# Six direct pairs instead of four in three feed-forwards of a decoder trunk, with slots handed on by age, two low parts moved to VectorE, and a norm's last squares added later

## The chip, the cores and the metric

The kernel runs on one core of one Trainium2 chip. The metric is the device time of one execution in microseconds (us); lower is better. The kernel before takes 1963.95 us, the median of 3 runs (1963.61 to 1965.31).

## What is computed

A two-layer decoder trunk on one sequence of 512 tokens with 1024 channels, in float32. Each layer is feed-forward, token mixer, feed-forward, each added to x behind a norm:

```python
def rms_norm(x, g):
    y = x * lax.rsqrt(jnp.mean(x * x, axis=-1, keepdims=True) + NORM_EPS)
    return y * g

def swiglu_ffn(x, g, w_in, w_out):          # w_in 1024 x 5632, w_out 2816 x 1024
    h = rms_norm(x, g)
    gate, up = jnp.split(h @ w_in, 2, axis=-1)
    return (jax.nn.silu(gate) * up) @ w_out

for layer in range(2):
    x = x + 0.5 * swiglu_ffn(x, ffn1_norm[layer], ffn1_w_in[layer], ffn1_w_out[layer])
    x = x + mixer(x)     # layer 0: retention beside dilated attention ("hybrid"); layer 1: stick-breaking ("stick")
    x = x + 0.5 * swiglu_ffn(x, ffn2_norm[layer], ffn2_w_in[layer], ffn2_w_out[layer])
return rms_norm(x, final_norm)
```

## The kernel before

**Layout and precision.** x is kept transposed in eight tiles `x[c]` of 128 channels x 512 tokens. Every operand of a matmul is cut in two parts, hi (a cast) and lo (what the cast left over), and a product is three matmuls: hi x hi, hi x lo, lo x hi (`mm3`). `split` makes hi on ScalarE (line 206) and lo on VectorE (line 207). Weights come by a DMA from SP's queue into a slot of the role `wraw`, and their two parts stand in two slots of the role `whl` (`weight`).

**Slots and roles.** The on-chip memory has 43 slots m0 to m42, of which `WSLOTS` (0 to 9) belong to the weights: four for `wraw`, six for `whl`. `give(role=[...])` hands a role a list of slots and starts its turn at 0; `B(shape, dtype, role)` takes the next slot in turn, and what is written there waits until the slot's last reader is done. Six `whl` slots hold three cut weights.

**Order.** Instructions are put in order ahead of time by a scheduler that goes by program order as priority; `tc.high_priority(offset=n)` moves a block ahead. Between `order["on"] = True` and `False` TensorE's instructions keep the order of the code. Each engine and each DMA queue then runs its list in that order.

**The stages.** A first feed-forward (`ffn`), `hybrid`, then three times `ffn_seven` and its output projection, with `stick` ahead of the third. "First, second and third stage" below are the three calls of `ffn_seven`, which begin near 625, 977 and 1594 us and end where the output projection begins, near 854, 1218 and 1831 us.

- `ffn_seven` computes the 22 gate tiles and 22 up tiles (128 channels each) and gate x up. The first `DIRECT` = 4 pairs are direct: for each f a gate tile into a bank of the kind `acc` (`pg`, three banks) and an up tile into one of the kind `att` (`pu`, four banks), each 24 matmuls of 512 columns on h. Their eight weights are the input `wd`. Those with an index in `BYDMA` (5, 6, 7: the up weights of f = 1, 2, 3) get lo from `weight_dma`: ScalarE casts hi and then writes -hi into lo, and an accumulating DMA from POOL's queue adds the source to it. h is x times a gain, not yet normalized; the norm's factor r (`rr`) is applied to the products. It needs the sum of squares `ss` and one matmul with `ones_ms` (`norm_r`), which stands behind the first gate tile.
- `normed_forms` makes on VectorE and ScalarE the seven sums of quarters of the normalized x (T3, T1, T4, B11, T2, B22, B21) that the quads multiply.
- The other 18 pairs run as 9 quads (`quad`): two pairs at a time, with their weights in four blocks a11, a12, a21, a22 (input `wq`), by seven products instead of eight. A product is 24 matmuls of 256 columns. The order is p3 x T3, p1 x T1, a22 x T4, a11 x B11, p2 x T2, p4 x B22, a12 x B21, where p1 to p4 are sums of blocks on VectorE. p1 to p4 are cut by `cut_form` (ScalarE and VectorE); a22, a11 and a12 by `cut_raw`, which like `weight_dma` gets lo from an accumulating DMA of POOL's queue (lines 459 to 461). For the quads `wraw` has `WSLOTS[:4]` and three more slots, and `whl` has `WSLOTS[4:]` and four slots of h.
- `out_ffn` multiplies by `w_out` in eight tiles d, each in three pieces of weights (p = 0, 8, 15). Between the pieces `cut_ahead` loads a later mixer's weight, cuts it and stores both parts to DRAM ("a cut ahead"). n cuts are spread over the eight tiles, 12 in the first projection and 16 in the second and the third (that of the layer-0 `ffn2` is the second). After each tile x[d] is updated and `norm_chunk` makes h[d] (hi on ScalarE, lo on VectorE) and adds its square to `ss`.
- `out_second` is the last part of a mixer's output projection: four tiles at a time, in two passes over its three input chunks. It too ends in `norm_chunk`.

Of the kernel before, what the change touches and what calls it, by code (L numbers as in the profile page):

```python
# [30 lines left out]
GN_EPS = 1e-5  # L31


@with_exitstack
def trunk(ctx: ExitStack, tc: tile.TileContext, a: dict, out: bass.AP):
# [18 lines left out]
    home = {"h": list(range(10, 18))}  # L54

# [191 lines left out]

    def norm_chunk(c, gcol, ss):
        norm_h(c, gcol)
        norm_sum(c, ss)  # L250
# [11 lines left out]
    def norm_r(ss, epsr=None):  # L262
        ps = PS("po")
        mm(ps, ones_ms, ss, start=True, stop=True)
        r = rstd(ps, NORM_EPS, eps_n, "r")
        if epsr is not None:
            nc.vector.tensor_scalar(out=epsr, in0=ps, scalar1=NORM_EPS, scalar2=GN_EPS, op0=ALU.add, op1=ALU.mult)
        return r
# [31 lines left out]
    def out_ffn(w_out, us, gcol, ahead, n):  # L300

        ss = norm_start()
        act_set(LNEXP)
        for d in range(KC):
            ps = ACC()
            m = n * (d + 1) // KC - n * d // KC
            out_tile(w_out[d], ps, us, then=lambda p: cut_ahead(*ahead.pop(0)) if p in (8, 15)[2 - m:] else None)
            add_half(d, ps)
            norm_chunk(d, gcol, ss)
        return ss  # L310
# [61 lines left out]
    def out_second(wb, chunks, gcol):  # L372

        ss = norm_start()
        for d0 in range(0, KC, 4):
            ws = [unit((wb, d0 // 2 + i), 768) for i in range(2)]
            ps = [ATT() for _ in range(4)]
            for f in ((0, 1), (2,)):
                for i in range(4):
                    for g in f:  # L380
                        mm3(ps[i], ws[i // 2], (i % 2) * 384 + g * P, chunks[5 + g][:, 0, :], chunks[5 + g][:, 1, :],
                            g == 0, g == 2)
            for i in range(4):
                nc.vector.tensor_add(out=x[d0 + i], in0=ps[i], in1=x[d0 + i])
                norm_chunk(d0 + i, gcol, ss)
        return ss
# [39 lines left out]
    DIRECT, FORMS_AT = 4, 3  # L426
    FIRST, BYDMA = 40, (5, 6, 7)
# [53 lines left out]
    def weight_dma(src, cols):  # L481
        raw = B((P, 1024), F32, "wraw")
        hi, lo = (B((P, 1024), F32R, "whl")[:, :cols] for _ in range(2))
        nc.sync.dma_start(raw[:, :cols], src)
        nc.scalar.copy(out=hi, in_=raw[:, :cols])
        nc.scalar.mul(out=lo, in_=f32(hi), mul=-1.0)
        nc.gpsimd.dma_start(lo, src, accum_op=ALU.add)
        return hi, lo

    def quad(wq, fm, uq):  # L490

# [14 lines left out]
        w = cut_raw(a22, wq[3])  # L506
# [3 lines left out]
        w = cut_raw(a11, wq[0])  # L510
# [27 lines left out]
    def ffn_seven(ss, wd, wq, gcol, ahead=[]):  # L538
# [8 lines left out]
        for f in range(DIRECT):  # L547
# [3 lines left out]
            else:  # L551
                w2 = [weight_dma(wd[i], D) if i in BYDMA else weight(wd[i], D) for i in (f, DIRECT + f)]
            pg = ACC()
            proj_tile(None, pg, w2[0])
            if f == 0:
                rr = norm_r(ss)
                act_set(SILU)
# [4 lines left out]
            pu = ATT()  # L562
            proj_tile(None, pu, w2[1])
# [5 lines left out]
            if f == FORMS_AT:  # L569
                fm = normed_forms(rr, gcol, ext + late[3:])  # L570
        give(wraw=WSLOTS[:4] + ext[:3], p3=ext[3:], whl=WSLOTS[4:] + old[4:])
        for q in range((FC - DIRECT) // 2):
            uqs.append(B((P, 2, SEQ), F32, "uq"))
            quad(wq[q], fm, uqs[-1])
        order["on"] = False
        give(u=forms + ext + old[4:])
# [5 lines left out]
        give(wraw=WSLOTS[:4], whl=WSLOTS[4:])  # L582
# [574 lines left out]
def _layout(i):  # L1157
# [21 lines left out]
    for n, w in enumerate((g("ffn2_w_in")[0], g("ffn1_w_in")[1], g("ffn2_w_in")[1])):  # L1179
        c = cols(w)  # L1180
        o[f"wd{n}"] = np.concatenate([c[:4], c[FC:FC + 4]])

        c = c.reshape(2, FC, P, 2, 512)[:, 4:].reshape(2, FC // 2 - 2, 2, P, 2, 512)
        o[f"wq{n}"] = np.ascontiguousarray(c.transpose(1, 0, 4, 3, 2, 5).reshape(FC // 2 - 2, 4, P, 2, 512))
# [52 lines left out]
```

## Time and profile before

| | |
|---|---|
| median of 3 runs | 1963.95 us (1963.61 to 1965.31) |
| the profiled execution | 1965.91 us, of which the span is 1964.2 us |
| instructions | 29107 |
| HBM | 296.58 MB read, 67.11 MB written, 185 GB/s over the span |
| accumulating DMAs of `wq`, POOL's queue | 81, of 512 KB |
| `wraw<-wq` / `wraw<-wd` / `wraw<-f_out`, SP's queue | 108 / 24 / 102 |

All rows shown here come from that one profiled execution. Times are in microseconds from the start of the span. A row of an engine's timeline reads: start, duration, engine, line, operation, output<-inputs, shape, how many of them in a row, and in brackets how long the engine stood idle before it and what ended that. A row of the chain that ended last reads: start, duration, what it spent the time on. A row of a table by windows reads: the window, its length, busy time of TensorE (PE), its weight load (PEld), VectorE (DVE), ScalarE (ACT) and GpSimd (POOL) with the number of instructions, then the granted clock of TensorE, the share of the DMA engines and GB/s. Ends of matmuls are modelled: the last of a row of them has a tail of some 0.16 us.

### The profile page before, as it was taken

Reading aid. Unit: us, or ns where it says so; the run is one execution under the profiler, and the core shown is the slowest. Engines: PE = TensorE matmul, PEld = TensorE weight load, DVE = VectorE, ACT = ScalarE, POOL = GpSimd, SP = SyncE. Lnnn points to the kernel's source line nnn. Section 1 sums busy time; section 2 is a strip of 40 time slices with the busy share of each in tenths; the row PEclk is TensorE's granted clock in tenths of the full one; section 3 lists DMA queues with packets and bytes.
Section 4 is the critical chain, followed back from the end, with each engine's and each line's share of the span. In section 5 each row is a group of like instructions: output and inputs, shape, how many; then the busy total and the mean of one; then the engine's idle time right before and its main releaser. Section 6 shows DMA issues by size and latency. Waiting matters only on the chain.

```text
span 1964.2 us, 29107 instructions
## 1 busy us (share of the span) xinstructions
PE 1927.4 (98%) x11288; PEld 1708.9 (87%) x11288; DVE 1270.2 (65%) x1809; ACT 1002.3 (51%) x1442; POOL 145.0 (7%) x260
## 2 busy tenths in 40 slices
PE   9999999999999999999998999999999998999998
PEld 7878888888887899988778999888889878999887
DVE  7565544347767976765476677443888877677534
ACT  5344333223566566663355667343666655666523
POOL 0000000001000011100001110000222200111000
PEclk9999999999999999999999999999999999999999
DMA  7787767877533777668757766878555455777433
GB/s 245 268 290 241 257 228 251 296 254 240 177 108 104 180 172 199 161 203 295 267 173 172 199 164 151 277 245 271 162 171 159 142 146 144 199 172 170 110 91 119
DMA packets 120362, 386.57 MB, mean 197 GB/s; under 512 B 14624, under 2 KB 16288, under 8 KB 120224
## 3 DMA queue, kind: packets, MB, share of 16 engines
q1 hardware_dynamic: 107120, 337.27, 51.8%
q0 software_dynamic: 12960, 47.19, 14.0%
q8 instruction: 88, 1.44, 0.3%
q14 instruction: 50, 0.41, 0.1%
q10 hardware_dynamic: 144, 0.26, 0.0%
HBM read 296.58 MB, written 67.11 MB: 185 GB/s over the span
## 4 chain that ended last, share of the span: by engine, by line
PE 82%; DMA 7%; DVE 5%; issue 3%; ACT 2%; POOL 0%; SPq 0%; DVEq 0%; ACTq 0%; POOLq 0%
PE acc L120 42%; PE att L120 38%; PE po L120 2%; DVE whl L207 2%; DMA wraw<-f_out 1%; DMA cut_sb_k<-whl 1%; DMA whl<-wq 1%; ACT whl L206 1%; DMA wraw<-hyb_g 1%; DMA wraw<-hyb_rq 1%; DMA cut_sb_q<-whl 1%; DMA wraw<-wd 1%; DMA centred<-wraw 1%; DMA cut_sb_v<-whl 0%; PE att L123 0%
## 5 line engine op out<-in xcount | busy, mean ns | idle before, releaser
L206 ACT CAST whl<-wraw 128x1024 fp32r<-128x1024 f32 (+4 forms) x323 | 316.6, 991 | 492.3 <-PE acc L120 198.4
L207 DVE TENSOR_TENSOR whl<-wraw,whl 128x1024 fp32r<-128x1024 f32 (+4 forms) x323 | 369.7, 1151 | 303.1 <-ACT whl L206 247.4
L120 PE MATMUL acc<-u,whl 128*128 128x512 f32 (+1 forms) x2244 | 483.5, 377 | 2.0 <-DVE whl L207 2.0
L120 PEld LDWEIGHTS acc<-u,whl 128*128 128x128 f32 x2244 | 403.2, 188 | 81.0 <-DVE whl L207 3.7
L120 PE MATMUL att<-fT,whl 128*128 128x256 f32 x2592 | 324.0, 285 | 12.1 <-DMA whl<-wq 11.4
L120 PEld LDWEIGHTS att<-fT,whl 128*128 128x128 f32 x2592 | 318.6, 194 | 13.0 <-DMA whl<-wq 11.8
L120 PE MATMUL acc<-h,whl 128*128 128x512 f32 x1248 | 303.2, 393 | 6.2 <-DVE whl L207 2.9
L120 PEld LDWEIGHTS acc<-h,whl 128*128 128x128 f32 x1248 | 232.6, 188 | 60.9 <-DVE h L238 5.3
L120 PE MATMUL att<-fB,whl 128*128 128x256 f32 x1944 | 242.4, 283 | 0.0
L120 PEld LDWEIGHTS att<-fB,whl 128*128 128x128 f32 x1944 | 237.6, 192 | 0.0
L120 PE MATMUL att<-h,whl 128*128 128x512 f32 x816 | 197.7, 395 | 3.6 <-DMA whl<-wd 3.6
L120 PEld LDWEIGHTS att<-h,whl 128*128 128x128 f32 x816 | 155.1, 190 | 38.7 <-DMA whl<-wd 4.0
L459 ACT CAST whl<-wraw 128x1024 fp32r<-128x1024 f32 x81 | 84.9, 1049 | 86.3 <-PE att L120 86.3
L461 POOL DMA_DIRECT2D whl<-wq x81 | 70.1, 866 | 498.6 <-ACT whl L460 263.4
L120 PE MATMUL acc<-h,wraw 128*128 128x512 f32 x432 | 104.8, 391 | 0.0
L120 PEld LDWEIGHTS acc<-h,wraw 128*128 128x128 f32 x432 | 80.0, 188 | 16.1
L207 DVE TENSOR_TENSOR whl<-p,whl 128x1024 fp32r<-128x1024 f32 x27 | 33.1, 1225 | 88.1 <-ACT whl L206 88.1
L460 ACT ACTIVATE whl<-whl 128x1024 fp32r<-128x1024 f32 x81 | 85.9, 1060 | 2.4
L936 POOL TENSOR_SCALAR_AFFINE_SELECT t<-t 128x128 f32<-128x128 f32 x128 | 46.3, 384 | 191.3 <-DVE t L953 125.1
L102 ACT ACTIVATE t<-t 128x512 f32<-128x512 f32 (+1 forms) x91 | 51.6, 587 | 6.7 <-DVE t L789 4.2
L297 DVE SCALAR_TENSOR_TENSOR x<-acc,x 128x512 f32<-128x512 f32 (+1 forms) x34 | 22.4, 659 | 48.8 <-PE acc L120 48.7
L206 ACT CAST whl<-p 128x1024 fp32r<-128x1024 f32 x27 | 28.3, 1048 | 48.4 <-PE att L120 33.0
(183 smaller groups left out, 2146.8 us busy)
## 6 DMA issues: line engine op xcount, KB each, us to landing
wraw<-wq SPq DMA_DIRECT2D x108, 512.0 KB, 5.5
whl<-wq POOLq DMA_DIRECT2D x81, 512.0 KB, 6.6
wraw<-f_out SPq DMA_DIRECT2D x68, 448.0 KB, 4.3
wraw<-f_in SPq DMA_DIRECT2D x42, 512.0 KB, 4.7
wraw<-f_out SPq DMA_DIRECT2D x34, 512.0 KB, 4.5
wraw<-wd SPq DMA_DIRECT2D x24, 512.0 KB, 4.3
cut_sb_q<-whl SPq DMA_DIRECT2D x16, 512.0 KB, 4.4
cut_sb_k<-whl SPq DMA_DIRECT2D x16, 512.0 KB, 4.8
```

Of the source, the lines that this page charges most:

```text
L102: r = nc.scalar.activation(out=o, in_=i, func=f, **kw)
L120: return ordered(nc.tensor.matmul(*args, **kw))
L206: nc.scalar.copy(out=hi, in_=src)
L207: nc.vector.tensor_tensor(out=lo, in0=src, in1=f32(hi), op=ALU.subtract)
L297: nc.vector.scalar_tensor_tensor(out=x[d][:, sl], in0=ps[:, sl], scalar=0.5, in1=x[d][:, sl], op0=ALU.mult, op1=ALU.add)
L459: nc.scalar.copy(out=hi, in_=raw)
L460: nc.scalar.mul(out=lo, in_=f32(hi), mul=-1.0)
L461: nc.gpsimd.dma_start(lo, src, accum_op=ALU.add)
L936: nc.gpsimd.affine_select(out=t[:, at:at + P], in_=t[:, at:at + P], pattern=[[1, P]], compare_op=ALU.is_gt, fill=0.0, base=0, channel_mult ...
```

## The change

- `DIRECT` goes from 4 to 6: six pairs are direct, and eight quads are left. The weights are laid out to match (`_layout`).
- `BYDMA` is empty and `weight_dma` is gone: every direct weight is cut by `weight`.
- In quad 0 of each call (`early`) a22 and a11 are cut by `cut_form` instead of `cut_raw`. a12 keeps `cut_raw`.
- Before the quads, and for `u` and the weights behind them, a role's slots are handed on in the order in which they come free (`oldest`) instead of from the first on.
- In `norm_chunk` the squares of the last four tiles are not added there but put on a list (`pending`), which `norm_r` works off.
- In `ffn_seven` the first up tile comes before `norm_r`.
- In `out_ffn` the n cuts ahead are spread over the first seven tiles, up to three in one; the last has none.
- In `out_second` the second four tiles go through all three chunks one after the other, and their update and h come with high priority.

```diff
+DIRECT = 6
...
+    def oldest(role):
+        n = turn_of[role] % len(roles[role])
+        return roles[role][n:] + roles[role][:n]
...
+    pending = []
+
     def norm_chunk(c, gcol, ss):
         norm_h(c, gcol)
-        norm_sum(c, ss)
+        if c < KC - 4:
+            norm_sum(c, ss)
+        else:
+            pending.append((c, ss))
...
     def norm_r(ss, epsr=None):
+        while pending:
+            norm_sum(*pending.pop(0))
         ps = PS("po")
...
         for d in range(KC):
             ps = ACC()
-            m = n * (d + 1) // KC - n * d // KC
-            out_tile(w_out[d], ps, us, then=lambda p: cut_ahead(*ahead.pop(0)) if p in (8, 15)[2 - m:] else None)
+            m = n * (d + 1) // (KC - 1) - n * d // (KC - 1) if d < KC - 1 else 0
+            out_tile(w_out[d], ps, us, then=lambda p: cut_ahead(*ahead.pop(0)) if p in (0, 8, 15)[3 - m:] else None)
...
-            for f in ((0, 1), (2,)):
+            for f in ((0, 1), (2,)) if d0 == 0 else ((0, 1, 2),):
...
             for i in range(4):
-                nc.vector.tensor_add(out=x[d0 + i], in0=ps[i], in1=x[d0 + i])
-                norm_chunk(d0 + i, gcol, ss)
+                with tc.high_priority(offset=2 * FIRST if d0 else 0):
+                    nc.vector.tensor_add(out=x[d0 + i], in0=ps[i], in1=x[d0 + i])
+                    norm_chunk(d0 + i, gcol, ss)
...
-    DIRECT, FORMS_AT = 4, 3
-    FIRST, BYDMA = 40, (5, 6, 7)
+    FIRST, BYDMA = 40, ()
...
-    def quad(wq, fm, uq):
+    def quad(wq, fm, uq, early):
+        raw = (lambda t, src: cut_form(t)) if early else cut_raw
...
-        w = cut_raw(a22, wq[3])
+        w = raw(a22, wq[3])
...
-        w = cut_raw(a11, wq[0])
+        w = raw(a11, wq[0])
...
             pg = ACC()
             proj_tile(None, pg, w2[0])
             if f == 0:
+                pu = ATT()
+                proj_tile(None, pu, w2[1])
                 rr = norm_r(ss)
                 act_set(SILU)
...
-            if f == FORMS_AT:
-                fm = normed_forms(rr, gcol, ext + late[3:])
-        give(wraw=WSLOTS[:4] + ext[:3], p3=ext[3:], whl=WSLOTS[4:] + old[4:])
+            if f == DIRECT - 1:
+                fm = normed_forms(rr, gcol, ext + late[DIRECT // 2:])
+        give(wraw=oldest("wraw") + ext[:3], p3=ext[3:], whl=oldest("whl") + old[4:])
         for q in range((FC - DIRECT) // 2):
             uqs.append(B((P, 2, SEQ), F32, "uq"))
-            quad(wq[q], fm, uqs[-1])
+            quad(wq[q], fm, uqs[-1], q == 0)
         order["on"] = False
-        give(u=forms + ext + old[4:])
+        ring, raws = oldest("whl"), oldest("wraw")
+        give(u=forms + [i for i in raws + ring if i not in WSLOTS] + ext[3:])
...
-        give(wraw=WSLOTS[:4], whl=WSLOTS[4:])
+        give(wraw=[i for i in raws if i in WSLOTS], whl=[i for i in ring if i in WSLOTS])
```

How the order of instructions moves, at three places. Numbers behind a name tell one tile from another and differ between the kernels.

TensorE at the start of the third stage, around the norm's matmul `po<-ss,ones_ms`; `acc` is the first gate tile (`pg`), `att` the first up tile (`pu`). Before:

```order
L120 MATMUL acc_15163<-h_15138,whl_15153 128x512
L120 MATMUL acc_15163<-h_15145,whl_15152 128x512 x2
L120 MATMUL acc_15163<-h_15145,whl_15153 128x512
L120 MATMUL po_15188<-ss_15000,ones_ms 128x512
L120 MATMUL att_15204<-h_15050,whl_15158 128x512 x2
```

Now:

```order
L126 MATMUL att_14978<-h_14934,whl_14949 128x512
L126 MATMUL att_14978<-h_14938,whl_14948 128x512 x2
L126 MATMUL att_14978<-h_14938,whl_14949 128x512
L126 MATMUL po_15015<-ss_14802,ones_ms 128x512
L126 MATMUL acc_15047<-h_14852,whl_15036 128x512 x2
```

The norm's matmul moved from behind the first gate tile to behind the first up tile.

ScalarE where the third stage goes from the direct tiles to quad 0. The casts of p3 and p1 come first, then the silu of the last direct pair (`t<-tp`), then the blocks: before, `wraw_15512` is a11 and `wraw_15513` is a22; now `wraw_15450` is a11 and `wraw_15451` is a22. Before:

```order
L206 CAST whl_15525<-p_2548_15519 128x1024
L206 CAST whl_15556<-wraw_15511 128x1024
L102 ACTIVATE t_15414<-tp_15412 128x512
L459 CAST whl_15616<-wraw_15512 128x1024
L460 ACTIVATE whl_15617<-whl_15616 128x1024
L459 CAST whl_15586<-wraw_15513 128x1024
L460 ACTIVATE whl_15587<-whl_15586 128x1024
```

Now, and with it VectorE's list at the same place (second fence), in which `p_2588` and `wraw_15680` are the sums p3 and p1 of quad 1:

```order
L212 CAST whl_15463<-p_2559_15457 128x1024
L212 CAST whl_15494<-wraw_15449 128x1024
L108 ACTIVATE t_15352<-tp_15350 128x512
L212 CAST whl_15553<-wraw_15450 128x1024
L212 CAST whl_15524<-wraw_15451 128x1024
L506 COPY t_15491<-att_15459 128x512
```
```order
L502 TENSOR_TENSOR p_2588_15688<-wraw_15681,wraw_15680 128x1024
L508 TENSOR_TENSOR wraw_15680<-wraw_15680,wraw_15682 128x1024
L567 TENSOR_TENSOR tp_15350<-acc_15325,r_15024 128x512
L213 TENSOR_TENSOR whl_15495<-wraw_15449,whl_15494 128x1024
L213 TENSOR_TENSOR whl_15554<-wraw_15450,whl_15553 128x1024
L574 TENSOR_TENSOR tp_15379<-att_15354,r_15024 128x512
L213 TENSOR_TENSOR whl_15525<-wraw_15451,whl_15524 128x1024
```

ScalarE's second pass for each block (line 460) is gone, and VectorE has the two subtractions instead, behind the two sums of quad 1.

SP's queue at the end of the second output projection, from the last tile's first piece of weights (`f_out`, 128x1024) on; `cut_sb_...<-whl` is a store of a cut ahead, `wd` the next stage's direct weights. Before:

```order
L148 DMA wraw_8681<-f_out 128x1024
L148 DMA wraw_8711<-f_out 128x896
L148 DMA wraw_8738<-sb_q 128x1024
L148 DMA wraw_8774<-sb_k 128x1024
L180 DMA cut_sb_k_8670<-whl_8665 128x1024
L180 DMA cut_sb_k_8670<-whl_8666 128x1024
L148 DMA wraw_8747<-f_out 128x896
L180 DMA cut_sb_q_8744<-whl_8739 128x1024
L148 DMA wraw_8790<-wd 128x1024
```

Now:

```order
L154 DMA wraw_8591<-f_out 128x1024
L154 DMA wraw_8621<-f_out 128x896
L186 DMA cut_sb_k_8583<-whl_8578 128x1024
L186 DMA cut_sb_k_8583<-whl_8579 128x1024
L154 DMA wraw_8679<-wd 128x1024
L154 DMA wraw_8685<-wd 128x1024
L154 DMA wraw_8648<-f_out 128x896
L154 DMA wraw_8773<-wd 128x1024
```

The last tile's two loads of later weights are gone from among its own, and the first two `wd` loads moved ahead of its last piece.

More of the change, by code (lines that the diff above doesn't have):

```diff
@@ L479, in product @@
                 mm(o, l, bh, start=False, stop=k == 3, skip_group_check=True)
[L481 to L488, printed above, removed]
-    def quad(wq, fm, uq):
+    def quad(wq, fm, uq, early):
+        raw = (lambda t, src: cut_form(t)) if early else cut_raw
         a21, a11, a22, a12 = (B((P, 2, SEQ), F32, "wraw") for _ in range(4))
@@ L551, in ffn_seven @@
             else:
-                w2 = [weight_dma(wd[i], D) if i in BYDMA else weight(wd[i], D) for i in (f, DIRECT + f)]
+                w2 = [weight(wd[i], D) for i in (f, DIRECT + f)]
             pg = ACC()
@@ L561, in ffn_seven @@
             func(s, t1, AF.Silu)
-            pu = ATT()
-            proj_tile(None, pu, w2[1])
+            if f:
+                pu = ATT()
+                proj_tile(None, pu, w2[1])
             t2 = T(tag="tp")
@@ L1180, in _layout @@
         c = cols(w)
-        o[f"wd{n}"] = np.concatenate([c[:4], c[FC:FC + 4]])
-        c = c.reshape(2, FC, P, 2, 512)[:, 4:].reshape(2, FC // 2 - 2, 2, P, 2, 512)
-        o[f"wq{n}"] = np.ascontiguousarray(c.transpose(1, 0, 4, 3, 2, 5).reshape(FC // 2 - 2, 4, P, 2, 512))
+        nq = (FC - DIRECT) // 2
+        o[f"wd{n}"] = np.concatenate([c[:DIRECT], c[FC:FC + DIRECT]])
+        c = c.reshape(2, FC, P, 2, 512)[:, DIRECT:].reshape(2, nq, 2, P, 2, 512)
+        o[f"wq{n}"] = np.ascontiguousarray(c.transpose(1, 0, 4, 3, 2, 5).reshape(nq, 4, P, 2, 512))
     w = g("hyb_w_in")[0]
```

## The prediction

> **What bounds the kernel now.** I read the busy times first, then the chain that ended last, then TensorE's own timeline for every piece of idle time, and last the stages around the largest pieces. The busy line says that TensorE is the bound, and that only waits in front of it, or a change in its own work, can move the time:
>
> ```profile
> PE 1927.4 (98%) x11288; PEld 1708.9 (87%) x11288; DVE 1270.2 (65%) x1809; ACT 1002.3 (51%) x1442; POOL 145.0 (7%) x260
> ```
>
> The chain gives TensorE's two speeds and the ends of the three `ffn_seven` calls (where the output projection begins):
>
> ```profile
> 251.27 125.12 PE acc L120 x552
> 675.71 178.58 PE att L120 x1486
> 854.29 34.49 PE acc L120 x153
> 1218.07 125.15 PE acc L120 x552
> 1830.95 100.58 PE acc L120 x486
> ```
>
> A matmul of 512 columns takes 125.12 / 552 = 0.2267 us, one of 256 columns 178.58 / 1486 = 0.1202 us. TensorE's timeline shows where each `ffn_seven` begins (its first `acc<-h`) and the waits in it, in brackets:
>
> ```profile
> 624.67 4.15 PE L120 MATMUL acc<-h,whl 128*128 128x512 f32 x16
> 629.42 0.96 PE L120 MATMUL acc<-h,whl 128*128 128x512 f32 x3 [0.60 <-DVE h L238]
> 675.71 5.78 PE L120 MATMUL att<-fT,whl 128*128 128x256 f32 x46 [0.73 <-DVE whl L207]
> ```
> ```profile
> 977.12 0.61 PE L120 MATMUL acc<-h,whl 128*128 128x512 f32 x2
> 978.76 5.32 PE L120 MATMUL acc<-h,whl 128*128 128x512 f32 x22 [1.02 <-DVE whl L207]
> 983.92 1.02 PE L120 MATMUL po<-ss,ones_ms 128*128 128x512 f32 x2
> 984.38 6.05 PE L120 MATMUL att<-h,whl 128*128 128x512 f32 x24
> 1010.82 8.03 PE L120 MATMUL att<-h,whl 128*128 128x512 f32 x22 [3.60 <-DMA whl<-wd]
> 1029.57 6.15 PE L120 MATMUL att<-fT,whl 128*128 128x256 f32 x50
> 1041.09 4.18 PE L120 MATMUL att<-fT,whl 128*128 128x256 f32 x22 [5.37 <-DMA whl<-wq]
> ```
> ```profile
> 1593.61 5.02 PE L120 MATMUL acc<-h,whl 128*128 128x512 f32 x21
> 1599.86 0.51 PE L120 MATMUL acc<-h,whl 128*128 128x512 f32 x1 [1.23 <-ACT h L237]
> 1600.90 0.73 PE L120 MATMUL acc<-h,whl 128*128 128x512 f32 x2 [0.54 <-DVE h L238]
> 1640.62 6.15 PE L120 MATMUL att<-fT,whl 128*128 128x256 f32 x50
> 1652.78 5.06 PE L120 MATMUL att<-fT,whl 128*128 128x256 f32 x22 [6.01 <-DMA whl<-wq]
> ```
>
> Without a wait such a stage would take 8 tiles x 24 x 0.2267 = 43.5, the norm's matmul 984.38 - 983.92 = 0.5, and 9 quads x 168 x 0.1202 = 181.7: together 225.7. It takes 854.29 - 624.67 = 229.6, 1218.07 - 977.12 = 240.9 and 1830.95 - 1593.61 = 237.3. The waits therefore cost 3.9, 15.2 and 11.6, together **30.7 us**. That is more than the brackets, because the clock falls after the long ones; the column behind the busy times is the granted clock (0.58, 0.70, 0.50):
>
> ```profile
> 1010.00:1018.00 8.00, 7.18 (x19) 5.68 (x20) 6.33 (x11) 5.77 (x10) 0.86 (x1) 0.58 0.88 279
> 1041.00:1046.00 5.00, 4.92 (x30) 4.92 (x31) 0.00 (x0) 0.81 (x1) 0.00 (x0) 0.70 1.05 309
> 1652.00:1658.00 6.00, 5.22 (x24) 5.22 (x25) 0.00 (x0) 0.33 (x1) 0.00 (x0) 0.50 0.92 277
> ```
>
> The 22 matmuls at 1010.82 took 8.03 where 22 x 0.2267 plus a tail of 0.16 is 5.15: 2.9 us lost to the clock behind a wait of 3.60. The Trainium skill (TensorE: Matmul & The Clock Gate, Part 1) has the clock halved after an idle window of some 3.4 us until about as long a busy one, an estimate of 1.7 us lost each time; the rows here show more, and the sum keeps the rows.
>
> **Where the two quad waits come from.** Let T0 be the end of the last direct tile (1029.57 in the second stage). The first two products of quad 0 run, then the third needs lo of a22. The slots of a22's halves are those of the last direct tile, so its cast starts only at T0, and lo comes by a second ScalarE pass and an accumulating transfer:
>
> ```profile
> 1029.78 1.03 ACT L459 CAST whl<-wraw 128x1024 fp32r<-128x1024 f32 x1
> 1030.85 1.06 ACT L460 ACTIVATE whl<-whl 128x1024 fp32r<-128x1024 f32 x1
> 1032.27 0.86 POOL L461 DMA_DIRECT2D whl<-wq  x1 [1.17 <-ACT whl L460]
> 1038.02 0.86 POOL L461 DMA_DIRECT2D whl<-wq  x1 [4.89 <-ACT whl L460]
> ```
> ```profile
> 1032.27 8.77 DMA whl<-wq
> ...
> 1643.32 9.43 DMA whl<-wq
> ...
> whl<-wq POOLq DMA_DIRECT2D x81, 512.0 KB, 6.6
> ```
>
> So lo lands 11.5 us after T0 (1041.04); TensorE needs it 48 x 0.1202 + 0.24 = 6.0 us after T0.
>
> **The change, part by part.**
>
> *Lo on VectorE (quad 0, and BYDMA empty).* The subtraction has a row, and the load on VectorE in this stage too (third busy time: 42.03 of 52 us):
>
> ```profile
> L207 DVE TENSOR_TENSOR whl<-wraw,whl 128x1024 fp32r<-128x1024 f32 (+4 forms) x323 | 369.7, 1151 | 303.1 <-ACT whl L206 247.4
> 1014.44 1.89 DVE L207 TENSOR_TENSOR fT<-tf,fT 128x512 fp32r<-128x512 f32 x3
> 977.00:1029.00 52.00, 47.38 (x194) 37.91 (x193) 42.03 (x58) 26.77 (x37) 2.62 (x3) 0.93 0.61 180
> ```
>
> Now lo of a22 is ready at T0 + 0.2 + 1.03 + 0.2 + 1.15 = T0 + 2.6, with VectorE's evacuation of the last tile (0.63) beside the cast: 3.4 us early. On VectorE the subtraction waits for ScalarE, and ScalarE for TensorE; behind it stand p2, p4 and their lo, needed from T0 + 11.5 on. In the direct stage VectorE gains 3 + 4 + 2 subtractions (10.4) and 6 passes of 1.89 / 3 = 0.63 (3.8), while the stage grows by 21.8: 56.2 of 73.8, 76% instead of 81%. The forms have that much longer too. The wait of 3.60 at 1010.82 is an accumulating transfer as well and goes with it. I cost all this at nothing. What is late next is a12, the one block of quad 0 still by transfer: its slot is free after the second product, in the second stage it was issued at T0 + 8.5, so by 6.6 to 9.4 it lands at T0 + 15.1 to 17.9, and TensorE wants it at 144 x 0.1202 + 0.24 = T0 + 17.5. I take 0.5 a stage, **+1.5**; ends 0 and 6 (the slowest of these rows would give 0.4 a stage; 2 leaves room for a slower one).
>
> *Six direct pairs.* One quad (168 x 0.1202 = 20.2) becomes four tiles (96 x 0.2267 = 21.8): +1.57 a stage, **+4.7**. SP issues four more `wd` loads and four fewer `wq` loads of the same 512 KB, POOL eight accumulates fewer, ScalarE eight passes fewer: free. By the Trainium skill (TensorE: Matmul & The Clock Gate, Back-to-back issue gap: N / 2.4 + 2.5 ns) the exchange is an estimated 20.7 against 18.3, +7.1 in all, and the forecast 1945.6. The rows (226.7 and 120.2 ns where the page has 215.8 and 109.2) disagree in level and in ratio, and the sum uses them.
>
> *Tail of the norm.* The last four squares leave VectorE's way in front of h, the second half of `out_second` finishes its banks 9 x 0.2267 = 2.0 us apart instead of 0.7, and the norm's matmul moves behind the up tile. So the last h is ready some 3 us after the projection, needed after 21 x 0.2267 = 4.8: the waits at 629.42, 1599.86 and 1600.90 go. r is begun a tile (5.44) later, 11.4 us into the stage; of three `acc` banks the first is wanted again after six tiles, at 33 us, and between lie two ScalarE and three VectorE passes of some 0.6 to 0.7 each, so nothing waits. In hybrid and stick VectorE keeps its order (lo of the last h, then the sum): nothing.
>
> *Slots by age.* Counting turns, before's restart at slot 0 was already the oldest in the second and third stage; in the first it put p1 on the last tile's pair, the wait of 0.73. Now all three stages are alike, with a22 on that pair. The u slots in new order are first used at u14, 42 x 0.2267 = 9.5 us into the projection: nothing.
>
> *Cuts ahead in seven tiles.* The last tile has none, so the next `wd` loads come early: the wait of 1.02 at 978.76 goes. But with 16 cuts two tiles have three. A tile reads 1408 KB, a cut moves 1536 KB; a tile takes 15.64 us. Two cuts need 293 GB/s, three need 394. Today's waits in the second projection, its mean rate, and the fastest 8 us there:
>
> ```profile
> 905.82 44.52 PE L120 MATMUL acc<-u,whl 128*128 128x512 f32 x195 [0.71 <-DVE whl L207]
> 956.17 5.06 PE L120 MATMUL acc<-u,whl 128*128 128x512 f32 x21 [0.40 <-DVE whl L207]
> 972.64 4.64 PE L120 MATMUL acc<-u,whl 128*128 128x512 f32 x19 [0.74 <-DVE whl L207]
> DMA packets 9768, 34.70 MB, mean 289 GB/s; under 512 B 1088, under 2 KB 1088, under 8 KB 9761
> 882.00:890.00 8.00, 8.00 (x37) 6.55 (x36) 5.25 (x6) 3.56 (x5) 0.00 (x0) 1.00 0.90 325
> ```
>
> At 325 GB/s a tile with three cuts lasts 19.0, 3.3 over; at 289, 21.3, 5.7 over. Prefetch covers some; I take 2.0 for each of the two, between none and 3.3, and drop the 0.74 of the last tile: **+3.3** (ends -2.0 and +10.7). The third projection has smaller cuts (at most 318 GB/s in one tile): **+0.5** (0 to 1.5). The first has at most two to a tile: nothing.
>
> **Sum:** -30.7 + 1.5 + 4.7 + 3.3 + 0.5 = -20.7. The profiled execution took 1965.91 (span 1964.2), 1.96 above the median of the three runs; taken off the median, 1963.95 - 20.7 = **1943.2 us**.
>
> **Rivals.**
> *The transfers become the bound in the projections* (for it: 289 GB/s with waits already; against: the waits are under 1 us and the rate reached 325). Each three-cut tile loses 5.7, long enough for the clock to fall (2.9 more, as at 1010.82): -30.7 + 1.5 + 4.7 + 17.2 + 0.5 = -6.8, 1957.
> *The quad wait moves from a22 to a12* or to another accumulate, as long as before with its clock (5.37 and 6.01, plus 1.4 and 2.3 by which the 22 matmuls behind them outlast 22 x 0.1202 + 0.14; mean 7.5, three times): -30.7 + 4.7 + 3.8 + 22.6 = +0.4, no change, 1964. Against: a12 is needed 11.5 us after a22.
> *Slower: VectorE is blocked in front of quad 0.* In the new order the two sums of quad 1's raw blocks stand ahead of lo of p1, a11 and a22; if quad 1's loads are late, VectorE stops there and TensorE behind it, one for one. It decides from (30.7 - 4.7 - 3.8) / 3 = 7.4 us late in each stage; at 10 us, 1972. Against: SP issues those loads ahead of quad 0's.
>
> **Chances.** Forecast 0.68, with its own range 1937 to 1952; transfers 0.17; wait moved 0.07; VectorE 0.08. The range 1936.5 to 1957 runs from all extra costs at nothing, today's projection waits gone too (-28), to the transfer rival. A difference under 0.2% (3.9 us) is about what a measurement of this kernel cannot tell from none. Faster 0.86, same 0.06, slower 0.08.
>
> **What would show it.** Right: no wait on `whl<-wd` or `whl<-wq` in front of `att`, clock 1.0 all through the three stages, each 227 to 229 us from first `acc<-h` to first `acc<-u`; waits of 1 to 3 us on `whl` in the fourth and seventh tile of the second projection. Wrong: waits over 3 us there with the clock down; a wait in quad 0's first or seventh product; direct tiles longer than 5.44.

## The result, and the profile after

The changed kernel takes 1945.38 us (median of 4 runs, 1943.44 to 1945.81), the kernel before 1964.63 us beside it (4 runs, 1963.61 to 1968.45): a ratio of 0.9897, 95% interval 0.9879 to 0.9914, some 19 us faster. Run once more beside its variants it took 1945.91 us (ratio 0.9908, 0.9895 to 0.9920). The profiled execution shown here took 1945.81 us, 20.1 us less than that of before.

The busy line of the profile after: TensorE has 216 matmuls fewer, VectorE as many instructions as before, ScalarE 39 fewer, POOL 24 fewer. The chain that ended last runs back over TensorE alone through the third stage: its eight quads in one piece without a release by another engine, where before the chain came from the transfer at 1652.78.

```profile
PE 1923.2 (99%) x11072; PEld 1697.0 (87%) x11072; DVE 1274.3 (66%) x1809; ACT 968.5 (50%) x1403; POOL 124.0 (6%) x236
...
1644.42 166.71 PE att L126 x1368
1811.14 100.58 PE acc L126 x486
```

The table by windows of the three stages, from the first `acc<-h` to the first `acc<-u` on TensorE's timeline, of before and then of after (columns as in the prediction; TensorE's granted clock is the third number from the end):

```profile
624.67:854.12 229.45, 227.43 (x1707) 217.58 (x1706) 176.23 (x212) 149.09 (x184) 26.06 (x30) 1.00 0.70 172
977.12:1217.90 240.78, 230.79 (x1707) 221.03 (x1706) 174.48 (x206) 146.92 (x179) 26.01 (x30) 0.98 0.69 172
1593.61:1830.79 237.18, 229.41 (x1707) 220.14 (x1706) 175.35 (x211) 149.41 (x184) 26.03 (x30) 0.99 0.69 168
```
```profile
625.61:854.10 228.49, 227.86 (x1635) 215.68 (x1634) 177.78 (x212) 136.44 (x168) 19.13 (x22) 1.00 0.61 157
977.70:1205.55 227.85, 227.70 (x1636) 215.76 (x1634) 171.91 (x203) 135.22 (x165) 19.09 (x22) 1.00 0.60 153
1583.52:1810.97 227.45, 227.45 (x1635) 215.71 (x1634) 177.15 (x211) 135.91 (x167) 19.10 (x22) 1.00 0.60 157
```

The stages give back 707.4 - 683.8 = 23.6 us, and TensorE is busy in nearly all of what is left. Cut at the same marks, the whole span reads as follows (the starts are those of TensorE's timeline; the columns e1 to e12 belong to the experiments below, each from its one profiled execution; e0 and e11 are given there in the text):

| us | before | after | e1 | e2 | e3 | e4 | e5 | e6 | e7 | e9 | e10 | e12 |
|---|---|---|---|---|---|---|---|---|---|---|---|---|
| first `ffn` | 251.1 | 250.7 | 250.5 | 250.2 | 250.6 | 248.9 | 249.8 | 249.1 | 249.1 | 249.7 | 250.6 | 250.2 |
| first projection | 119.7 | 121.4 | 123.6 | 121.7 | 119.7 | 123.5 | 119.7 | 121.5 | 121.9 | 119.7 | 119.7 | 124.2 |
| `hybrid` | 253.9 | 253.4 | 253.5 | 253.4 | 253.9 | 253.9 | 253.5 | 253.6 | 253.6 | 253.4 | 253.5 | 253.4 |
| first stage | 229.5 | 228.5 | 236.7 | 233.2 | 228.4 | 228.8 | 231.0 | 232.7 | 230.9 | 234.1 | 230.2 | 228.5 |
| second projection | 123.0 | 123.6 | 125.8 | 129.1 | 123.6 | 123.7 | 122.5 | 124.0 | 127.1 | 122.9 | 122.6 | 121.9 |
| second stage | 240.8 | 227.8 | 235.8 | 231.1 | 228.0 | 227.6 | 233.4 | 228.6 | 235.8 | 232.5 | 233.2 | 231.1 |
| third projection | 119.7 | 122.6 | 123.4 | 120.0 | 119.7 | 122.4 | 119.7 | 121.7 | 124.4 | 119.7 | 119.7 | 119.7 |
| `stick` | 256.0 | 255.4 | 255.4 | 255.4 | 255.4 | 255.3 | 255.5 | 255.4 | 255.4 | 255.3 | 255.4 | 255.4 |
| third stage | 237.2 | 227.5 | 235.7 | 231.0 | 227.5 | 227.5 | 228.5 | 233.2 | 235.2 | 234.2 | 230.5 | 227.5 |
| last projection and norm | 133.4 | 133.1 | 133.2 | 132.7 | 133.1 | 132.6 | 132.6 | 132.9 | 137.6 | 132.6 | 132.6 | 132.7 |

So from before to after: stages -23.6, the three projections 362.4 to 367.6, +5.3, everything else -1.8.

TensorE's timeline of after at the start of quad 0 in the second stage, where before had the wait of 5.37: the last direct tile, then the seven products without a bracket. The two rows behind it are ScalarE's cast of a22 and VectorE's lo of it:

```profile
1038.44 5.60 PE L126 MATMUL att<-h,whl 128*128 128x512 f32 x24
1043.88 8.79 PE L126 MATMUL att<-fT,whl 128*128 128x256 f32 x72
1052.51 3.04 PE L126 MATMUL att<-fB,whl 128*128 128x256 f32 x24
```
```profile
1043.89 1.05 ACT L212 CAST whl<-wraw 128x1024 fp32r<-128x1024 f32 x1 [0.80 <-PE att L126]
1044.97 1.23 DVE L213 TENSOR_TENSOR whl<-wraw,whl 128x1024 fp32r<-128x1024 f32 x1
```

lo of a22 is there at 1046.2, T0 + 2.3, where the transfer of before brought it at T0 + 11.5.

What waits now are the projections. TensorE's timeline of after, the six waits of over 0.5 us in the three projections, in order:

```profile
362.96 9.37 PE L126 MATMUL acc<-u,whl 128*128 128x512 f32 x40 [1.46 <-DVE whl L213]
...
911.41 8.93 PE L126 MATMUL acc<-u,whl 128*128 128x512 f32 x37 [1.58 <-DVE whl L213]
961.78 0.73 PE L126 MATMUL acc<-u,whl 128*128 128x512 f32 x2 [0.64 <-ACT whl L212]
963.05 14.81 PE L126 MATMUL acc<-u,whl 128*128 128x512 f32 x64 [0.54 <-DVE whl L213]
1287.50 20.05 PE L126 MATMUL acc<-u,whl 128*128 128x512 f32 x87 [0.78 <-DVE whl L213]
1308.16 10.49 PE L126 MATMUL acc<-u,whl 128*128 128x512 f32 x45 [0.61 <-DVE whl L213]
```

and ScalarE's timeline ahead of the first, the second and the fifth of them, where a cast stands 5 to 7 us on a slot whose old content, a cut ahead, is still being stored (`cut_...<-whl`). Before the second, another cast comes in between, at 907.20, and waits 2.39 us on a store too:

```profile
358.71 1.78 ACT L212 CAST whl<-wraw 128x896 fp32r<-128x896 f32 x2 [6.72 <-DMA cut_sb_v<-whl]
...
901.77 1.90 ACT L212 CAST whl<-wraw 128x896 fp32r<-128x896 f32 x2 [6.15 <-DMA cut_sb_v<-whl]
...
1284.22 1.57 ACT L212 CAST whl<-wraw 128x640 fp32r<-128x640 f32 x2 [5.23 <-DMA cut_sb_oa<-whl]
```

Toward the end of these three waits the DMA engines are full for 3 to 4 us (the last two numbers are their share and GB/s):

```profile
356.00:359.00 3.00, 3.00 (x15) 2.49 (x14) 0.34 (x1) 0.29 (x1) 0.00 (x0) 1.00 1.01 400
899.00:903.00 4.00, 4.00 (x19) 3.33 (x18) 0.83 (x2) 1.23 (x2) 0.00 (x0) 1.00 1.00 397
1282.00:1285.00 3.00, 3.00 (x15) 2.46 (x14) 0.00 (x0) 0.78 (x2) 0.00 (x0) 1.00 1.02 389
```

### The profile page after: what moved, and what is told of

The parts are those of the page before. It is cut to its first block, busy times and chain, and to the rows that moved or that the text cites. A ratio compares the mean times of both kernels' runs of the same rounds, so it can differ in the third digit from the quotient of the medians.

```text
span 1944.1 us, 28582 instructions
## 1 busy us (share of the span) xinstructions
PE 1923.2 (99%) x11072; PEld 1697.0 (87%) x11072; DVE 1274.3 (66%) x1809; ACT 968.5 (50%) x1403; POOL 124.0 (6%) x236
## 5 line engine op out<-in xcount | busy, mean ns | idle before, releaser
L213 DVE TENSOR_TENSOR whl<-wraw,whl 128x1024 fp32r<-128x1024 f32 (+4 forms) x341 | 392.0, 1155 | 296.3 <-ACT whl L212 254.5
L126 PE MATMUL acc<-h,whl 128*128 128x512 f32 x1392 | 336.0, 393 | 1.4 <-DVE whl L213 1.3
L126 PEld LDWEIGHTS acc<-h,whl 128*128 128x128 f32 x1392 | 260.1, 188 | 60.0 <-DVE whl L213 3.4
L126 PE MATMUL att<-fT,whl 128*128 128x256 f32 x2304 | 284.3, 283 | 0.0
L126 PEld LDWEIGHTS att<-fT,whl 128*128 128x128 f32 x2304 | 280.1, 192 | 0.2
L126 PE MATMUL att<-h,whl 128*128 128x512 f32 x960 | 226.8, 390 | 1.5 <-ACT whl L212 0.8
L126 PE MATMUL att<-fB,whl 128*128 128x256 f32 x1728 | 215.6, 283 | 0.1
L126 PEld LDWEIGHTS att<-h,whl 128*128 128x128 f32 x960 | 180.1, 188 | 40.1 <-ACT whl L212 1.5
L126 PEld LDWEIGHTS att<-fB,whl 128*128 128x128 f32 x1728 | 210.9, 192 | 0.4 <-DMA whl<-wq 0.4
L213 DVE TENSOR_TENSOR u<-uq,u 128x512 fp32r<-128x512 f32 x66 | 44.3, 688 | 10.2 <-ACT u L212 9.8
```

The costliest lines, as they stand in the source:

```text
L126: return ordered(nc.tensor.matmul(*args, **kw))
L213: nc.vector.tensor_tensor(out=lo, in0=src, in1=f32(hi), op=ALU.subtract)
```

## The experiments

Theory: the 20 us are the quad waits, removed by lo on VectorE; the rest of the change is small, its price 4.7 us for the exchanged quads and some 4 in the projections. The rivals are in each expectation. All times are medians of 4 to 12 runs, ratios are against the kernel before on the same chip, with their 95% intervals. Waits and stages are those of the one profiled execution, which can lie some us from the median (e1's was the longest of its runs).

**e0, the changed kernel again**

> The changed kernel once more, beside its variants on the same chip: 1945.4 us, with waits of TensorE of 14.3 us in all or less, none of them in a quad. What differs by under 1 us between this run and the first tells how small a difference the variants can show.

1945.91 us. Stages 229.1, 228.1 and 227.5; in quad 0 two short waits on a12's transfer (0.46 and 0.35 us), where none was expected. TensorE's waits add up to 13.3 us (12.1 in the first execution), within the 14.3 expected. The projections took 121.2, 125.4 and 122.7 us: the second, 123.6 in the first execution of the same kernel, can differ by 1.8 us from one execution to the next. e0 ran beside e1, e2 and e3 on the same chip, so they are compared with this number.

**e1, lo of a22 and a11 by transfer again**

```diff
-            quad(wq[q], fm, uqs[-1], q == 0)
+            quad(wq[q], fm, uqs[-1], False)
```

> The changed kernel, but quad 0 of each stage gets lo of a22 and a11 by the ScalarE pass and the accumulating transfer again. Theory (lo on VectorE removed the quad waits): a wait of 5 to 6 us on whl<-wq in front of the third product of quad 0 comes back in all three stages, the first too, since a22 now stands on the last direct tile's slots there as well; with the clock behind it 5.37 + 1.4 and 6.01 + 2.3, mean 7.5, three times: +15 to +23 us, some 1963. Rival (the six direct pairs give the quads' weights enough room, and VectorE's part is not needed): no wait there, within 2 us of the changed kernel, 1945.

1969.05 us, +23.1 against e0; ratio 1.0028 (1.0018 to 1.0037), slower than before. TensorE's timeline has one wait in the quads of each stage, ahead of the third product of quad 0:

```profile
706.48 5.06 PE L126 MATMUL att<-fT,whl 128*128 128x256 f32 x22 [5.75 <-DMA whl<-wq]
...
1067.94 5.07 PE L126 MATMUL att<-fT,whl 128*128 128x256 f32 x22 [5.59 <-DMA whl<-wq]
...
1682.41 5.06 PE L126 MATMUL att<-fT,whl 128*128 128x256 f32 x22 [5.47 <-DMA whl<-wq]
```

and the stages are 8.2, 8.0 and 8.2 us longer than in after: 5.6 of wait and 2.3 of clock (22 x 0.1202 + 0.14 = 2.78 took 5.06). The first stage has it too, since slots by age put a22 on the last tile's pair there. The theory holds, at its upper end.

**e5, the kernel before with that one edit**

```diff
-            quad(wq[q], fm, uqs[-1])
+            quad(wq[q], fm, uqs[-1], q == 0)
```

(with the lines of `quad` that take the new argument, as in the change)

> The kernel before with one edit: quad 0 of each stage cuts a22 and a11 by ScalarE and VectorE, as the changed kernel does. Theory (the two quad waits of 5.37 and 6.01 and the clock behind them come from the accumulating transfers alone): -15 us (5.37 + 1.4 + 6.01 + 2.3), 1949, and no wait in quad 0. Rival (with four direct pairs VectorE has no room for two more subtractions there): a wait of 2 to 5 us on whl comes in their place, -10 to 0 us.

1947.57 us; ratio 0.9906 (0.9892 to 0.9919): the theory, at 2 us more than its size. That is the ratio of the whole change within the intervals. By stages: 229.5 to 231.0 (three waits of 0.55 to 0.63 in and behind quad 0), 240.8 to 233.4, 237.2 to 228.5. The wait on `whl<-wd` in the second stage stayed (3.11 us). Everything else in the change together adds some 2 us to what this edit gives, which the intervals don't tell from nothing.

**e2, four direct pairs**

```diff
-DIRECT = 6
+DIRECT = 4
```

> The changed kernel with four direct pairs (DIRECT = 4) and nine quads; all else as changed. Theory (an exchanged quad costs 1.57 us and the two more direct pairs are not needed for anything else): -4.7 us, some 1940.5. Rival (with four pairs VectorE does not get through the sums, the forms of x and the twelve subtractions in time, 81% and more of that time being taken): a wait of over 2 us in quad 0 of each stage on fT or whl, which with the clock falling costs more than 4.7: 1947 to 1960.

1963.1 us, +17.2 against e0; ratio 0.9992 (0.9982 to 1.0002). The rival: the exchange of quads that the prediction priced as a cost of 4.7 carries 17 us. TensorE's timeline where quad 0 of the second stage begins (the first and the third stage have the same two brackets, 1.90 and 1.28), VectorE's sum that p3 is made of, and the window ahead of it:

```profile
1033.98 0.50 PE L126 MATMUL att<-fT,whl 128*128 128x256 f32 x2 [1.90 <-ACT whl L212]
1035.76 4.44 PE L126 MATMUL att<-fT,whl 128*128 128x256 f32 x23 [1.28 <-DVE whl L213]
```
```profile
1031.02 1.21 DVE L502 TENSOR_TENSOR p<-wraw,wraw 128x1024 f32<-128x1024 f32 x1
```
```profile
1000.00:1032.00 32.00, 32.00 (x142) 26.21 (x140) 31.77 (x48) 16.68 (x26) 0.00 (x0) 1.00 0.37 115
```

VectorE is busy 31.77 of 32.00 us from the making of r on, and the sum for p3 begins at 1031.02, a microsecond before TensorE needs what is cut from it. In after the stretch between the same two points is this:

```profile
990.00:1044.00 54.00, 54.00 (x241) 44.69 (x240) 47.67 (x64) 24.02 (x34) 0.00 (x0) 1.00 0.35 108
```

47.67 of 54.00. So r a tile later and every lo on VectorE leave it no room with four pairs; two more pairs of direct tiles give it. In this one execution the stages lost 11.5 us against after's and the second projection 5.5; the median lies 3.6 us above that execution's 1959.47, and what the others lost more is not shown.

**e9, four pairs with r a tile earlier**

```diff
-DIRECT = 6
+DIRECT = 4
...
-            m = n * (d + 1) // (KC - 1) - n * d // (KC - 1) if d < KC - 1 else 0
+            m = n * (d + 1) // KC - n * d // KC
...
             if f == 0:
-                pu = ATT()
-                proj_tile(None, pu, w2[1])
                 rr = norm_r(ss)
...
-            if f:
-                pu = ATT()
-                proj_tile(None, pu, w2[1])
+            pu = ATT()
+            proj_tile(None, pu, w2[1])
```

> The changed kernel with the cuts ahead over eight tiles, four direct pairs, and the norm's matmul behind the first gate tile again, so that r comes a tile (5.44 us) earlier; the last squares stay on the list. Theory (with four pairs the quads started 3.2 us late only because VectorE, busy 31.77 of the 32.00 us before them, began a tile late): no wait of over 1 us in quad 0; 1940.1 - 4.7 + 1 to 2 for squares that are late at the start of a stage: 1936 to 1938. Rival (VectorE has no room for four pairs however early r is, since the subtractions of quad 0 are new there): waits of 1 to 3 us in quad 0 with the clock down, 1942 to 1955.

1955.93 us; ratio 0.9948 (0.9935 to 0.9962). The time is just above the rival's range (1942 to 1955), but the cause is not the rival's: in front of quad 0's first products the wait is 0.92 at most where e2 had 1.90 and 1.28, so the later r was most of what VectorE lacked. The price moved to the norm's matmul (TensorE's timeline, third stage):

```profile
1597.30 2.04 PE L126 MATMUL po<-ss,ones_ms 128*128 128x512 f32 x2 [4.32 <-DVE ss L252]
```

The sum of squares is 4.32 us late (3.86 in the first stage), because VectorE cuts the direct weights ahead of it. The second stage also waited 2.57 us for a12.

**e6, the tail of the norm as before**

```diff
-        if c < KC - 4:
-            norm_sum(c, ss)
-        else:
-            pending.append((c, ss))
+        norm_sum(c, ss)
...
-            for f in ((0, 1), (2,)) if d0 == 0 else ((0, 1, 2),):
+            for f in ((0, 1), (2,)):
...
-                with tc.high_priority(offset=2 * FIRST if d0 else 0):
+                with tc.high_priority(offset=0):
...
             if f == 0:
-                pu = ATT()
-                proj_tile(None, pu, w2[1])
                 rr = norm_r(ss)
...
-            if f:
-                pu = ATT()
-                proj_tile(None, pu, w2[1])
+            pu = ATT()
+            proj_tile(None, pu, w2[1])
```

> The changed kernel with the tail of the norm as before: the last squares added at once, the second four tiles of out_second in two passes, the norm's matmul behind the first gate tile. Theory (the tail was worth its waits at 629.42, 1599.86 and 1600.90 and no more): +2 to +4 us, 1947.5 to 1949.5, with waits on h in the first gate tile of the first and the third stage. Rival (r a tile earlier gives VectorE room that is worth something): 0 or less.

1955.5 us; ratio 0.9954 (0.9941 to 0.9966), some 10 us slower than after. The direction of the theory, more than twice its size: TensorE waits on h for 0.37 and 1.01 us in the first stage and not in the third, but the larger wait is one that before did not have, for `ss`, 2.86 in the first stage and 3.83 in the third (TensorE's timeline):

```profile
1596.01 1.99 PE L126 MATMUL po<-ss,ones_ms 128*128 128x512 f32 x2 [3.83 <-DVE ss L252]
```

e6 takes back three edits at once; in e9, with four pairs, where the late squares and the new order of `out_second` stay, the norm's matmul behind the gate tile waits as long (3.86 and 4.32), so it is the place of the matmul that gives the sum its time. That the wait comes from lo on VectorE is argued and not shown alone: in the third stage of e6 two subtractions for direct weights stand between the last three squares, and e5, where three of these lo still come by transfer, has no wait on `ss`. In after the last squares of the first stage are added at 634.45 + 1.41 = 635.9 and the matmul begins at 637.41; behind the gate tile it would have stood at 631.97 (TensorE's and VectorE's timelines of after):

```profile
631.97 5.60 PE L126 MATMUL att<-h,whl 128*128 128x512 f32 x24
637.41 1.02 PE L126 MATMUL po<-ss,ones_ms 128*128 128x512 f32 x2
```
```profile
634.45 1.41 DVE L252 TENSOR_TENSOR ss<-ss,t 128x512 f32<-128x512 f32 x2
```

**e7, slots from the first on**

```diff
-        give(wraw=oldest("wraw") + ext[:3], p3=ext[3:], whl=oldest("whl") + old[4:])
+        give(wraw=WSLOTS[:4] + ext[:3], p3=ext[3:], whl=WSLOTS[4:] + old[4:])
...
-        ring, raws = oldest("whl"), oldest("wraw")
-        give(u=forms + [i for i in raws + ring if i not in WSLOTS] + ext[3:])
+        give(u=forms + ext + old[4:])
...
-        give(wraw=[i for i in raws if i in WSLOTS], whl=[i for i in ring if i in WSLOTS])
+        give(wraw=WSLOTS[:4], whl=WSLOTS[4:])
```

> The changed kernel with slots handed on from the first on, as before, instead of by age. Theory (the old order was already by age in two stages): 0 to +0.7 us, 1945 to 1947. Rival (with six direct pairs the first slot is no longer the oldest in any stage, and handing on by age is needed): a wait in each stage where the quads begin or where the projection begins, +3 to +10 us.

1971.92 us; ratio 1.0033 (1.0020 to 1.0045), 26 us slower than after. The rival, at more than twice its price. TensorE's timeline at both places in the second stage:

```profile
1050.18 0.51 PE L126 MATMUL att<-fT,whl 128*128 128x256 f32 x2 [1.41 <-ACT whl L212]
1052.61 7.60 PE L126 MATMUL att<-fT,whl 128*128 128x256 f32 x49 [1.93 <-DVE whl L213]
```
```profile
1218.26 1.21 PE L126 MATMUL acc<-u,whl 128*128 128x512 f32 x4 [2.89 <-ACT whl L212]
1221.23 5.06 PE L126 MATMUL acc<-u,whl 128*128 128x512 f32 x11 [1.76 <-DVE whl L213]
```

For the second stage the turn explains it: the projection ahead of it cuts 24 + 16 = 40 weights; with 8 direct ones that makes 96 halves, a multiple of the six slots, so the first slot was the oldest. With 12 it makes 104, two past a multiple of six, and p3 gets the pair of the last direct tile, which is still running. The third stage has the same two brackets at its quads (1.41 and 1.93).

**e3, the cuts ahead over eight tiles**

```diff
-            m = n * (d + 1) // (KC - 1) - n * d // (KC - 1) if d < KC - 1 else 0
+            m = n * (d + 1) // KC - n * d // KC
```

> The changed kernel with the cuts ahead spread over all eight tiles of a projection again (two to a tile in the second). Theory (three cuts to a tile is what TensorE waits for in the projections): the waits of 1.46, 1.58, 0.78, 0.61 in the middle of the projections go, those of up to 1 us at the start of the next stage come back (1.02 before): -4 to -1 us, some 1942. Rival (the middle waits are only moved): the last tiles of a projection and the next stage's first weights wait for 3 to 5 us in all, and the time is 1945 to 1948.

1940.1 us, -5.8 against e0; ratio 0.9875 (0.9861 to 0.9890), the fastest of all. The first and the third projection lose their waits altogether (119.7 each). At the start of the second stage no wait came back, though it is there in the four-pair kernels with cuts in the last tile (0.92 in e9, 0.90 in e10). The second projection keeps 123.6 us, with one wait of 2.00 and a clock of 0.66 in the 5 us behind it (shown below). Against e5 the intervals do not overlap: the rest of the change is worth some 6 us on top of the one edit (0.9875 against 0.9906), and the seven tiles take most of that away again.

**e4, lo of three direct weights by transfer again**

```diff
-    FIRST, BYDMA = 40, ()
+    FIRST, BYDMA = 40, (7, 8, 9)
...
-                w2 = [weight(wd[i], D) for i in (f, DIRECT + f)]
+                w2 = [weight_dma(wd[i], D) if i in BYDMA else weight(wd[i], D) for i in (f, DIRECT + f)]
```

(with `weight_dma` as it was before)

> The changed kernel with lo of three direct up weights (f = 1, 2, 3) by the accumulating transfer again. Theory (those transfers waited only where cuts ahead stood in the last tile, and there are none now): 0, 1944 to 1947, no wait on whl<-wd. Rival (an accumulating transfer at the start of a stage is late in the second stage however the cuts stand): the wait of 3.1 to 3.6 us comes back there with the clock behind it, +4 to +7 us, 1950 to 1952.

1944.71 us; ratio 0.9897 (0.9883 to 0.9912): 0. No wait on `whl<-wd`, stages 228.8, 227.6 and 227.5. With six pairs and no cuts in the last tile, this part of the change is worth nothing that shows.

**e10, four pairs, r late, three lo by transfer** (e3 with `DIRECT = 4` and `BYDMA = (5, 6, 7)`)

> Cuts ahead over eight tiles, four direct pairs, the norm's matmul behind the first up tile, and lo of three direct up weights by the accumulating transfer, which takes three subtractions (3.5 us) from VectorE. Theory (the quads of the four-pair version started 3.2 us late for VectorE's work alone): no wait in front of quad 0; 1940.1 - 4.7 = 1935.4, and 3 to 6 more where the transfer is late in the second stage: 1935 to 1941. Rival (the subtractions are not what VectorE was late by; the passes for the forms, which can't begin before r, are): the 1.90 and 1.28 of each stage stay, 1950 to 1958.

1950.64 us; ratio 0.9924 (0.9907 to 0.9941). The time is in the rival's range, the wait is in between: at the start of quad 0 it falls from 3.18 to 1.54 us in each stage, and others of 0.3 to 1.5 follow in the quads, where VectorE and ScalarE are still behind. No wait on `whl<-wd`. Four pairs stay dearer than six.

**e11, the stores of the cuts by POOL's queue** (on e3)

```diff
-            nc.sync.dma_start(keep[:, i, :], f32(part[:, :cols]))
+            nc.gpsimd.dma_start(keep[:, i, :], f32(part[:, :cols]))
```

> The version with the cuts ahead over eight tiles, but the stores of the cuts go by POOL's queue instead of SP's. What is asked: why a projection waits where cuts ahead stand. Theory A (the DMA engines are full there, as the prediction had it): the same bytes, the same waits, 1939 to 1941. Theory B (ScalarE's cast stands 6 to 7 us on a slot that a cut's store still holds, and the store stands in SP's queue behind loads or holds up loads behind it): the second projection loses its wait of 2.00, 123.6 us becomes 120 to 121.5, and the whole 1936.5 to 1938.5. Theory C (stores by POOL's queue land later, as its accumulating transfers do): waits grow, over 1941.

2007.03 us, 67 above e3; ratio 1.0215 (1.0200 to 1.0230). By the time it is theory C; the three projections took 131.1, 155.9 and 134.6 us. Rows for the second projection of e3, then the same of e11: stores (median time from issue to landing last), what ScalarE's casts waited for, and what SP's queue waited for with its loads of weights (us in all, times, longest):

```profile
cut_sb_k<-whl SPq DMA_DIRECT2D x12, 512.0 KB, 5.5
...
ACT whl L212 <- DMA wraw<-f_out: 14.8, 4, 5.7
...
ACT whl L212 <- DMA cut_sb_k<-whl: 9.7, 5, 3.8
...
SPq L154 <- DVE whl L213: 40.3, 21, 3.8
```
```profile
cut_sb_k<-whl POOLq DMA_DIRECT2D x12, 512.0 KB, 6.3
...
ACT whl L212 <- DMA wraw<-f_out: 47.5, 6, 8.9
ACT whl L212 <- DMA cut_sb_k<-whl: 31.9, 5, 6.9
...
SPq L154 <- DVE whl L213: 113.9, 39, 10.8
```

These stores land 0.8 us later after their issue (those of q and v 1.2 later), and ScalarE stands on them three times as long. But its waits on loads of `w_out` grow by more, from 14.8 to 47.5, and SP's queue waits 113.9 us instead of 40.3 until VectorE is done with the slots that its loads go to. TensorE's waits there go from 2.0 to 23.5 us, while the projection moves 222 GB/s instead of 278. So a projection can wait while it moves less on the mean. How the 67 us divide between late stores and late loads is not shown, so theory C's mechanism is not shown either, and e11 does not decide between A and B: the DMA engines are full for stretches, and the part of the rate stays open.

**e12, 14, 14 and 16 cuts** (on e3)

```diff
-    ss = out_ffn(a["f1_out"][0], us, 8, hyb + sb[:4], 12)
+    ss = out_ffn(a["f1_out"][0], us, 8, hyb + sb[:6], 14)
...
-    ss = out_ffn(a["f2_out"][0], us, 24, sb[4:20], 16)
+    ss = out_ffn(a["f2_out"][0], us, 24, sb[6:20], 14)
```

> The version with the cuts ahead over eight tiles, with two cuts moved from the second projection to the first (14, 14 and 16 instead of 12, 16 and 16). Theory (a projection waits when cut follows cut at two to a tile for several tiles, so that ScalarE's cast comes to a slot whose store is still under way; a tile with one cut lets the queue recover): the second projection goes from 123.6 us to 120 to 121.5, the first from 119.7 to at most 120.5: -3 to -1 us, some 1938. Rival (the two cuts cost the same wherever they stand): the waits move to the first projection, 1939 to 1942.

1943.15 us; ratio 0.9883 (0.9867 to 0.9900), not to be told from e3 by the intervals. The theory's gain did not come. The profile speaks for the rival: the first projection loses 4.5 us, and the second stage begins with a new wait of 2.60 on h; the second projection's 1.7 us less is no more than it differs between two executions of one kernel (e0).

## Where the prediction was right and where not

The forecast of 1943.2 us stands 2.2 under the median of 1945.38 and rests on the right mechanism, but two of its terms were not what they seemed. That it comes so near is in part luck: the stages gave 23.6 us where it had 24.5, the projections cost 5.3 where it had 3.8, and other parts gave 1.8 that it did not have.

- *The waits of 30.7 us go.* Right. The stages took 683.8 us where no wait at all would give 3 x 227.3 = 681.9. e1 and e5 show the quad waits from both sides, +23.1 and -17.
- *Six direct pairs, +4.7.* The size was right as arithmetic: a stage without waits grew from 225.7 to 227.3. Its reading as a bare cost was wrong. The prediction worked out that VectorE goes from 81% to 76%, and did not price what VectorE would lack without the two pairs; without them (e2) the time is 17 us longer, not 4.7 shorter.
- *The tail of the norm: the waits on h go, nothing waits for r.* Right, and again the cover was not priced. With the rest of the change, the old tail waits 3 to 4 us for `ss` in the first and the third stage (e6).
- *Slots by age, 0.73 in one stage.* Right against before. Not seen: with 12 direct weights the turn shifts by two slots, and without the edit the change would have lost 26 us (e7).
- *a12, +1.5.* Too much: after has no wait there, e0 0.46 and 0.35 us.
- *The projections, +3.8.* The sum was near (+5.3) and its parts were not: the first lost 1.8 where I said nothing, the second 0.6 where I said 3.3, the third 2.9 where I said 0.5 with an end of 1.5. In e0 the second lost 2.4, so its 0.6 is not to be read finely. The step that failed is the price by mean transfer rate of a tile with three cuts. The first projection has no such tile, and waited. Its rows show ScalarE's cast behind a store that holds a slot; over the 8 us around it the rate is 250 to 262 GB/s, yet toward its end the DMA engines are full for 3 us, at 400. So a tile's mean rate does not tell where a projection waits; slot and short full stretch stand together in the rows, and no run parts them. The waits did come in the fourth tile and at the end of the seventh of the second projection, at 1.58 and 1.2 us.
- *No cuts in the last tile, so that the wait of 1.02 goes.* It went, but it also went with cuts in the last tile (e3), and the seven tiles cost 5.8 us. With six pairs, this part of the change loses.
- *Not in the sum:* -1.8 us in the other parts, 0.6 of it in `stick`; and a wait of 0.63 at the start of the first stage, for lo of a gate weight.
- *Two readings.* The prediction says that its rows show more than 1.7 us lost to the clock each time; they show 2.9, 1.4 and 2.3. The low end of its range, written 1936.5, is 1936.0 by its own sum (1963.95 - 28).

The rivals: the quad wait did not move to a12, VectorE was not blocked by quad 1's sums (they stand without a wait in all three stages), and the projections did not grow by the 17.2 of the transfer rival. The clock was 1.00 through all three stages.

## What to carry to other kernels

Price the parts of a change against each other and not only against the kernel before: here one edit gave 17 of 19 us by itself, and the rest of the change together added some 2; yet three parts of that rest cost 10 to 26 us each when taken out of the whole. When work is moved to an engine, add up its busy time in the stretch between the release of that work and its first use; a tile that looks like a cost on the bounding engine may be the room in which the other engine finishes. A ring of slots that is restarted at its first member is right only as long as the count of what went through it is a multiple of its length.

## What the chip showed that I had not expected

The clock falls after shorter waits than those of before, and not after every one. Windows from the end of a wait: 1.67 in e4 and 2.00 in e3, both in a projection; then 2.07 in e0, in a projection, and 2.86 in e6, at the norm's matmul of the first stage:

```profile
361.60:366.60 5.00, 4.96 (x15) 3.93 (x16) 0.59 (x1) 0.00 (x0) 0.00 (x0) 0.66 0.85 259
```
```profile
905.50:910.50 5.00, 5.00 (x15) 4.02 (x16) 0.94 (x1) 0.39 (x1) 0.00 (x0) 0.66 0.91 290
```
```profile
911.10:916.10 5.00, 4.97 (x21) 3.87 (x21) 2.01 (x2) 2.11 (x2) 0.00 (x0) 1.00 1.00 392
```
```profile
634.60:639.60 5.00, 4.97 (x20) 3.82 (x21) 2.29 (x4) 2.60 (x3) 0.00 (x0) 1.00 0.36 105
```

After 1.67 and 2.00 the clock is 0.66 over 5 us, a loss of 1.7 us that doubles the price of the wait; after 2.07 and 2.86 it is 1.00, so the length of the wait alone does not decide it. Cut to where it is down in e3, the clock is at half for 3.4 us:

```profile
905.56:908.96 3.40, 3.40 (x8) 2.73 (x9) 0.88 (x1) 0.00 (x0) 0.00 (x0) 0.50 0.94 267
```

The Trainium skill (TensorE: Matmul & The Clock Gate, Part 1) has the clock halved after an idle window of some 3.4 us. The half speed and the 3.4 us agree with this row; the waits ahead of it were half as long here.
